# ConvFFN 0's shift and scale and the spectrum's cross products on VectorE, the sums in other steps

## The chip, the cores and the metric

The kernel runs on one core of a Trainium2 chip. The metric is the device time of one execution in microseconds; the figure for the kernel before is the median of three runs.

A core has TensorE (PE in the profile; its weight loads are PEld), VectorE (DVE), ScalarE (ACT), GpSimd (POOL) and SyncE (SP), which here only issues DMAs. Each engine works through its own queue in order.

## What is computed

The reference is two layers over 512 tokens of width 1024, in float32. Layer 0 mixes by a Hyena long convolution (512 channels) beside neighbourhood attention (8 heads of 64, with 256 context tokens); layer 1 by a Conformer convolution. Each is followed by a ConvFFN, and each sub-layer is wrapped in norms with shift, scale and gate computed from a conditioning vector:

```
def adaln_params(cond, w_mod, b_mod):
    m = jax.nn.silu(cond) @ w_mod + b_mod
    return jnp.split(m[:, None, :], 6, axis=-1)
...
    shift1, scale1, gate1, shift2, scale2, gate2 = adaln_params(c, w_mod[layer], b_mod[layer])
    ...
    h = h + gate1 * rms_norm(y, g_mix_post[layer])
    hn = rms_norm(h, g_ffn_pre[layer]) * (1 + scale2) + shift2
    y = conv_ffn(hn, ffn_w_up[layer], ffn_w_dw[layer], ffn_b_dw[layer], ffn_w_down[layer])
...
def bidirectional_fft_conv(v, h_fwd, h_bwd, bias):
    ...
    v_f = jnp.fft.rfft(v.astype(jnp.float32), n=n, axis=1)
    k_f = jnp.fft.rfft(k_full, n=n, axis=0)
    y = jnp.fft.irfft(v_f * k_f[None], n=n, axis=1)[:, :length]
```

The change concerns `shift2` and `scale2` of layer 0 and the complex product `v_f * k_f`.

## The kernel before

**Numbers.** Every float32 product of weight and activation is made of three matmuls (`mm3`, lines 296 to 299) from a high and a low part of each operand. `split` (lines 311 to 316) makes the two parts of a loaded weight: ScalarE copies the high part (L314), VectorE subtracts it (L315).

**Loads.** Weights are read 512 KB at a time by `load` (line 306, DMA issued by SP at L308) into a pool `raw` of three buffers, and split into a pool `w` of eight; a `Stream` asks for the loads and splits some units ahead. The same three `raw` buffers take the loads of the background work.

**Stages around the change,** as the program is written: four key projections (`k_proj`, TensorE, keys evicted by L975 on ScalarE and L976 on VectorE) with two spectra between them (`fdft`); the value projection (four weights of 512 KB, two of them followed by the load and split of an inverse-transform table `ti`); the inverse transform (`py`, L1096 and L1098 on VectorE); two of the four query projections; then the attention, 16 units (`a_scores`, `a_exp`, `a_norm`, `a_T`, `a_split`, `a_pv`), with the other two query projections in it. GpSimd adds the bias tiles (L1135) and scales the softmax (L1180) there. The output projection and the second stage's transposes (L537), which use the ConvFFN's shift and scale (L548), follow.

**The spectrum's product** (`prod` in `fdft`, lines 992 to 1020): ScalarE copies the odd half from PSUM (L994, L995), VectorE forms sums and differences `v` (L998 to L1001), and for each of two halves the product with the filter's spectrum is two instructions of 128x1024: the cross product `tm` (L1007) on GpSimd, the direct one `yy` (L1008) on VectorE. VectorE combines them (L1011, L1012, L1017) and ScalarE and VectorE split the result (L1018, L1019).

**The shift and scale** (`mod_cols`, lines 455 to 473, which runs `gemv_acc`, lines 431 to 453) is a generator that advances only when `bg_step` is called. For layer 0 it has 27 steps: one load; 16 steps which each issue the next load and add one loaded block, times a column of SiLU(c), to `acc`; eight empty steps; one with 16 small matmuls `pm` (L465); one for the columns (L469 to L471). With `side=True` the block is scaled by ScalarE into a tile `gt` (L446) and added by GpSimd (L448); otherwise VectorE does both in one instruction (L452), as for the other layer and the gates. The steps are called three at a time: twice before and once after the second key projection, after each later key projection, after the second spectrum, and after each of the four weights of the value projection, so that all 27 are called before the inverse transform.

**What sets the order.** The program is handed to a scheduler that gives each engine's queue its order by a simulated timeline, with the written order as priority; a buffer is granted when the last reader of the tile in it is done. Only TensorE's order in the prologue is written out by hand.

Of the kernel before, what the change touches and what calls it, by code (L numbers as in the profile page):

```python
# [10 lines left out]
F32 = mybir.dt.float32  # L11
F32R = mybir.dt.float32r
AF = mybir.ActivationFunctionType
ALU = mybir.AluOpType
AX = mybir.AxisListType

P = 128
# [235 lines left out]
def backbone_kernel(ctx: ExitStack, tc: tile.TileContext, a, cols, out, dump=None, stop=None, mark=lambda s: None):  # L253
# [18 lines left out]
    def s4(dt=F32, shape=(P, 2, 512), n="s"):  # L272
        return spool.tile(list(shape), dt, name=nm(n), tag="s")
# [154 lines left out]

    MOD = {}

    def gemv_acc(src, n, cs, init=None, side=False):
        rs = []

        def ld(k):
            rs.append(load(src[k]))

        acc = s4(F32, (P, 1024), "acc")
        ld(0)
        yield None
        for k in range(n):  # L440
            if k < n - 1:
                ld(k + 1)
            ck_ = cs[:, k:k + 1]
            if side:
                t_ = acc if k == 0 else s4(F32, (P, 1024), "gt")
                A.activation(t_, rs[k], AF.Copy, bias=0.0, scale=ck_)  # L446
                if k:
                    G.tensor_tensor(acc, acc, t_, op=ALU.add)  # L448
            elif k == 0 and init is None:
                V.tensor_scalar(acc, rs[k], ck_, None, op0=ALU.mult)  # L450
            else:
                V.scalar_tensor_tensor(acc, rs[k], ck_, init if k == 0 else acc, op0=ALU.mult, op1=ALU.add)  # L452
            yield acc

    def mod_cols(l, whichs, side=False):

        n = 2 * len(whichs)
        acc = None
        for acc in gemv_acc(a[f"wcol{l}"], 8 * n, scn[n], side=side):
            yield  # L460
        for _ in range(8):
            yield
        pm = ps("pm")
        for m in range(8):
            PE.matmul(pm[:, n * m:n * m + n], acc[:, m * P:(m + 1) * P], sel[n], start=True, stop=True)  # L465
        yield
        for i, which in enumerate(whichs):
            B_, s_, A_ = col8(), col8(), col8()
            V.tensor_tensor(B_, pm[:, 2 * i:8 * n:n], pc(f"bsh{which}{l}"), op=ALU.add)  # L469
            V.tensor_tensor(s_, pm[:, 2 * i + 1:8 * n:n], pc(f"bsc{which}{l}"), op=ALU.add)  # L470
            V.scalar_tensor_tensor(A_, s_, 1.0, pc(f"gmp{l}" if which == 1 else f"gfp{l}"), op0=ALU.add, op1=ALU.mult)  # L471
            MOD[(l, which)] = (A_, B_)
        yield
# [27 lines left out]
    def bg_step(n=1):  # L501
        for _ in range(n):
            while bg:
                try:
                    next(bg[0])
                    break
                except StopIteration:
                    bg.pop(0)
# [442 lines left out]
                ctx_T()  # L951
        V.tensor_tensor(pp[i // 2][:, i % 2], got[0], got[1], op=ALU.mult)
    bg_drain()
    bg += [mod_cols(0, (2,), True)]


    mark("kproj")
# [24 lines left out]
    def fdft(fc):  # L982
        q4 = {}
        for par in (1, 0):
            for cs in range(2):
                pm = ps("pv")
                for hf in range(2):
                    ch = par * 2 + hf
                    mm3(pm, tfs(0, ch, cs, fc), tfs(1, ch, cs, fc), pT[0][:, ch], pT[1][:, ch], hf == 0, hf == 1)
                q4[(cs, par)] = pm  # L990

        def prod():
            od = s4(n="od")
            A.copy(od[:, 0], q4[(0, 1)])  # L994
            A.copy(od[:, 1], q4[(1, 1)])  # L995
            v0 = s4(n="v0")
            v1 = s4(n="v1")
            V.tensor_tensor(v0[:, 0], q4[(0, 0)], od[:, 0], op=ALU.add)  # L998
            V.tensor_tensor(v0[:, 1], q4[(1, 0)], od[:, 1], op=ALU.add)
            V.tensor_tensor(v1[:, 1], q4[(0, 0)], od[:, 0], op=ALU.subtract)  # L1000
            V.tensor_tensor(v1[:, 0], q4[(1, 0)], od[:, 1], op=ALU.subtract)  # L1001
            y = []
            for pr, v in ((0, v0), (1, v1)):
                kt = K[(fc, pr)]
                yy = s4(n="yy")
                tm = od if pr else s4(n="ytm")
                G.tensor_tensor(tm, v, kt[:, 1:2].broadcast_to([P, 2, 512]), op=ALU.mult)  # L1007
                V.tensor_tensor(yy, v, kt[:, 0:1].broadcast_to([P, 2, 512]), op=ALU.mult)  # L1008
                y.append((yy, tm))
            for yy, tm in y:  # L1010
                V.tensor_tensor(yy[:, 0], yy[:, 0], tm[:, 1], op=ALU.add)  # L1011
                V.tensor_tensor(yy[:, 1], yy[:, 1], tm[:, 0], op=ALU.subtract)  # L1012
            eh, el = p8(n="Eh"), p8(n="El")
            (y0, _), (y1, _) = y
            for j, (op, s) in enumerate(((ALU.add, 0), (ALU.add, 1), (ALU.subtract, 0), (ALU.subtract, 1))):
                X = (v0 if j < 2 else v1)[:, j % 2]
                V.tensor_tensor(X, y0[:, s], y1[:, 1 - s], op=op)  # L1017
                A.copy(eh[:, j], X)  # L1018
                V.tensor_tensor(el[:, j], X, f(eh[:, j]), op=ALU.subtract)  # L1019
            E[fc] = (eh, el)  # L1020
        return prod

    bg_step(3)
    ev0 = k_proj(0)
    p_T(3)
    bg_step(3)
    ev0()
    ev1 = k_proj(1)
    ev1()
    bg_step(3)  # L1030
    pr0 = fdft(0)
    pr0()
    mark("fdft")
    ev2 = k_proj(2)
    ev2()
    bg_step(3)
    ev3 = k_proj(3)
    ev3()
    bg_step(3)
    pr1 = fdft(1)  # L1040
    pr1()
    bg_step(3)


    mark("vproj")
# [2 lines left out]
    for kp in range(4):  # L1048
        wh, wl = ws.get(2, 2)
        for q in range(2):  # L1050
            kc = 2 * kp + q
            ns = slice(q * 512, (q + 1) * 512)
            for c in range(6):
                if c < 4:
                    sl = slice(c * P, (c + 1) * P)
                    ah, al = hk(hT, kc, 0, sl), hk(hT, kc, 1, sl)
                else:
                    sl = slice((c - 4) * P, (c - 3) * P)
                    ah, al = ck(kc, 0, sl), ck(kc, 1, sl)
                mm3(vacc[c], ah, al, wh[:, ns], wl[:, ns], kc == 0, kc == 7)  # L1060
        if kp in (1, 2):
            TI[kp - 1] = split(load(a["ti"][kp - 1]), None)
        bg_step(3)

    Vt = {}
    for c in range(6):
# [16 lines left out]
    for m in range(4):  # L1083
        py = ps("py")
        ms = slice(m * P, (m + 1) * P)
        for par in range(2):
            o = py[:, par * 256:(par + 1) * 256]
            for fc in range(2):
                for cs in range(2):
                    ns = slice(cs * 512 + par * 256, cs * 512 + par * 256 + 256)  # L1090
                    eh, el = E[fc]
                    j = par * 2 + cs
                    mm3(o, eh[:, j, ms], el[:, j, ms], TI[fc][0][:, ns], TI[fc][1][:, ns],
                        fc == 0 and cs == 0, fc == 1 and cs == 1)
        pi = pp[m // 2][:, m % 2]
        V.scalar_tensor_tensor(pi.rearrange("p (i e) -> p i e", e=2), pi.rearrange("p (i e) -> p i e", e=2),  # L1096
                               pc("hyb", m), py.rearrange("p (e i) -> p i e", e=2), op0=ALU.mult, op1=ALU.add)
        V.tensor_tensor(yh[m // 2][:, m % 2], pi, x0[m // 2][:, m % 2], op=ALU.mult)  # L1098

    mark("qproj")  # L1100

# [2 lines left out]
    def q_proj(pr):  # L1104
        u = ws.get(1, 2)
        pz = ps("pz")
        for kc in range(8):
            wh, wl = wst(u, kc)
            mm3(pz, wh, wl, hk(hT, kc, 0), hk(hT, kc, 1), kc == 0, kc == 7)
        t_, l_ = s4(F32R, n="qX"), s4(F32R, n="qL")  # L1110
        qX.append(t_)
        qL.append(l_)
        for e in range(2):
            G.memset(f(l_[HALF[1 - e], e]), 0.0)
        for e in range(2):
            src = pz[HALF[e]]
            for r in range(2):
                A.mul(t_[HALF[r], e], src, 0.125)
            V.scalar_tensor_tensor(l_[HALF[e], e], src, 0.125, f(t_[HALF[e], e]), op0=ALU.mult, op1=ALU.subtract)
# [104 lines left out]
    for u in range(16 + DV + 1):  # L1224
        if u < 16:
            a_scores(u)
            a_exp(u)
        if 2 <= u < 4:
            q_proj(u)
        if DN <= u < 16 + DN:  # L1230
            a_norm(u - DN)
        if DT <= u < 16 + DT:
            a_T(u - DT)
            a_split(u - DT)
        if DV <= u < 16 + DV:
            a_pv(u - DV)
        if u > DV and (u - DV) % 2 == 0:
            a_out((u - DV) // 2 - 1)
        if u == 2:
            v_shift()  # L1240
        if u % 4 < 2 and u < 12:
            bm_load(u // 4 * 2 + u % 4 + 2)
        if u % 4 in (1, 2) and u < 12:
            bm_make(u // 4 * 2 + u % 4 + 1)
# [305 lines left out]
```

## Time and profile before

| | before |
|---|---|
| median of 3 runs | 1291.08 us (1290.09 to 1294.53) |
| the profiled execution | 1290.61 us |
| its span, first to last instruction | 1288.8 us |
| busy: TensorE / VectorE / ScalarE / GpSimd | 1249.9 / 817.3 / 526.8 / 160.2 us |
| mean granted TensorE clock | 0.994 |
| chain that ended last | TensorE 76%, DMA 8%, VectorE 7%, ScalarE 4% |

The span is the part of an execution that the trace covers; the rest lies before the first and behind the last instruction. Times in the trace count from the span's start. A matmul's listed duration overlaps with the next one's, so TensorE's pace is read from the starts. Weight tiles are named `w`, the value projection's PSUM tiles `va`, the inverse transform's `py`, the key and query projections' `pz`.

### The profile page before, as it was taken

The numbers are of one execution on the slowest core, as the hardware profiler recorded it, in microseconds if no ns is written. First come the engines' busy times: TensorE is split into PE (matmuls) and PEld (weight loads), VectorE is DVE, ScalarE is ACT, GpSimd is POOL, SyncE is SP. The second block draws the span as 40 slices with busy tenths as digits, with TensorE's granted clock in tenths as the row PEclk, the third lists the DMA queues.
The fourth block names the chain that finished last, engine by engine and source line by source line (L and its number), as shares of the span: only waits on it lengthen the run. The fifth ranks groups of instructions, "written<-read, shape, count | busy, mean of one in ns | idle before, by whom it ended". The sixth has DMA issues, their size and how long they took to land.

```text
span 1288.8 us, 15592 instructions
## 1 busy us (share of the span) xinstructions
PE 1249.9 (97%) x6044; PEld 1027.3 (80%) x6044; DVE 817.3 (63%) x1068; ACT 526.8 (41%) x804; POOL 160.2 (12%) x198
## 2 busy tenths in 40 slices
PE   6999979999999999999999999999999999999997
PEld 3688867877898888878888887878888888888886
DVE  4577588476557888877825565686677555556233
ACT  5453543286435333243514433242544333345221
POOL 3210365283010000000000100101100000000001
PEclk9999998999999999999999999999999999999999
DMA  9536533342506477766336052040255333232321
GB/s 354 179 115 181 162 115 131 129 121 83 163 1 190 169 230 244 237 210 207 107 105 196 25 185 73 1 147 1 66 167 187 98 94 95 98 97 99 98 83 65
DMA packets 47818, 171.00 MB, mean 133 GB/s; under 512 B 5757, under 2 KB 5788, under 8 KB 47744
## 3 DMA queue, kind: packets, MB, share of 16 engines
q1 hardware_dynamic: 47092, 168.49, 39.9%
q0 software_dynamic: 464, 1.19, 0.4%
q8 instruction: 47, 0.77, 0.2%
q10 hardware_dynamic: 188, 0.33, 0.1%
q14 instruction: 27, 0.22, 0.1%
HBM read 167.10 MB, written 2.10 MB: 131 GB/s over the span
## 4 chain that ended last, share of the span: by engine, by line
PE 76%; DMA 8%; DVE 7%; ACT 4%; issue 3%; POOL 1%; SPq 0%; DVEq 0%; POOLq 0%; ACTq 0%
PE pz L297 12%; PE pz L298 12%; PE pz L299 12%; PE acc L297 8%; PE acc L298 8%; PE acc L299 8%; DMA raw<-in_wup 3%; DMA raw<-in_wcol 3%; DVE w L315 2%; PE pg L297 2%; PE pg L298 2%; PE pg L299 2%; ACT w L314 2%; PE po L1206 1%; PE pt L1186 1%
## 5 line engine op out<-in xcount | busy, mean ns | idle before, releaser
L299 PE MATMUL pz<-hTh,w 128*128 128x512 f32 (+1 forms) x920 | 345.2, 376 | 0.5 <-DVE w L315 0.5
L297 PE MATMUL pz<-hTh,w 128*128 128x512 f32 (+1 forms) x920 | 344.6, 377 | 0.9 <-DVE hTh L543 0.5
L298 PE MATMUL pz<-hTl,w 128*128 128x512 f32 (+1 forms) x920 | 345.4, 376 | 0.0
L315 DVE TENSOR_TENSOR w<-raw,w 128x1024 fp32r<-128x1024 f32 x159 | 201.1, 1268 | 211.1 <-ACT w L314 206.8
L314 ACT CAST w<-raw 128x1024 fp32r<-128x1024 f32 x159 | 166.3, 1051 | 345.5 <-PE pz L298 128.6
L299 PEld LDWEIGHTS pz<-hTh,w 128*128 128x128 f32 x920 | 173.8, 189 | 32.2 <-DVE w L315 1.0
L297 PEld LDWEIGHTS pz<-hTh,w 128*128 128x128 f32 x920 | 173.0, 189 | 31.5 <-DVE hTh L543 1.0
L298 PEld LDWEIGHTS pz<-hTl,w 128*128 128x128 f32 x920 | 173.9, 189 | 30.2 <-DVE hTl L544 0.4
L298 PE MATMUL acc<-w,gs 128*128 128x512 f32 x256 | 99.6, 389 | 0.0
L299 PE MATMUL acc<-w,gs 128*128 128x512 f32 x256 | 98.3, 389 | 0.0
L297 PE MATMUL acc<-w,gs 128*128 128x512 f32 x256 | 97.0, 389 | 0.0
L452 DVE SCALAR_TENSOR_TENSOR acc<-raw,sc,acc 128x1024 f32<-128x1024 f32 x59 | 75.6, 1281 | 28.6 <-DMA raw<-in_wgate 19.6
L416 POOL TENSOR_SCALAR t<-t,t 128x1 f32<-128x1 f32 x19 | 6.6, 348 | 636.6 <-ACT py L425 628.2
L901 ACT ACTIVATE cv<-pz,pk 128x512 f32<-128x512 f32 x88 | 67.6, 774 | 0.0
L903 DVE SCALAR_TENSOR_TENSOR cv<-pz,pk,cv 128x511 f32<-128x511 f32 x88 | 65.6, 747 | 1.8
L902 DVE SCALAR_TENSOR_TENSOR cv<-pz,pk,cv 128x511 f32<-128x511 f32 x88 | 65.2, 744 | 0.2 <-ACT cv L901 0.2
L1283 ACT ACTIVATE cv<-cv 128x512 f32<-128x512 f32 x44 | 27.7, 629 | 81.2 <-DVE cv L903 81.1
L297 PEld LDWEIGHTS acc<-w,gs 128*128 128x128 f32 x256 | 48.1, 188 | 10.1
L299 PEld LDWEIGHTS acc<-w,gs 128*128 128x128 f32 x256 | 48.1, 188 | 9.9
L298 PEld LDWEIGHTS acc<-w,gs 128*128 128x128 f32 x256 | 48.1, 188 | 9.9
L315 DVE TENSOR_TENSOR wk<-raw,wk 128x1024 fp32r<-128x1024 f32 x30 | 37.1, 1246 | 28.9 <-ACT wk L314 28.9
L558 DVE TENSOR_TENSOR py<-acc,gg 128x512 f32<-128x512 f32 x32 | 21.8, 688 | 48.4 <-ACT py L425 48.4
(334 smaller groups left out, 2050.2 us busy)
## 6 DMA issues: line engine op xcount, KB each, us to landing
raw<-in_wup SPq DMA_DIRECT2D x88, 512.0 KB, 3.6
raw<-in_wcol SPq DMA_DIRECT2D x48, 512.0 KB, 4.4
raw<-in_wdn SPq DMA_DIRECT2D x44, 512.0 KB, 3.6
raw<-in_wgate SPq DMA_DIRECT2D x32, 512.0 KB, 4.3
raw<-in_pw SPq DMA_DIRECT2D x24, 512.0 KB, 4.7
raw<-in_win SPq DMA_DIRECT2D x20, 512.0 KB, 3.6
land<-in_wmod SPq DMA_DIRECT2D x16, 512.0 KB, 10.2
raw<-in_wout SPq DMA_DIRECT2D x8, 512.0 KB, 3.6
```

Source lines behind the costliest of these rows:

```text
L297: PE.matmul(o, ah, bh, start=start, stop=False)
L298: PE.matmul(o, ah, bl, start=False, stop=False)
L299: PE.matmul(o, al, bh, start=False, stop=stop)
L314: A.copy(hi, r)
L315: V.tensor_tensor(lo, r, f(hi), op=ALU.subtract)
L452: V.scalar_tensor_tensor(acc, rs[k], ck_, init if k == 0 else acc, op0=ALU.mult, op1=ALU.add)
L558: V.tensor_tensor(p_[:, sl], y2[i], gg[:, sl], op=ALU.mult)
L901: A.activation(dst, pz, AF.Identity, bias=pc(bk, i), scale=pc(wk + "1", i))
L902: V.scalar_tensor_tensor(dst[:, 1:w], pz[:, 0:w - 1], pc(wk + "0", i), dst[:, 1:w], op0=ALU.mult, op1=ALU.add)
L903: V.scalar_tensor_tensor(dst[:, 0:w - 1], pz[:, 1:w], pc(wk + "2", i), dst[:, 0:w - 1], op0=ALU.mult, op1=ALU.add)
L1186: PE.transpose(b["pt"][:, c * P:(c + 1) * P], b["P"][:, c * P:(c + 1) * P], ident)
L1283: A.activation(cv[:, 0], cv[:, 0], AF.Silu, bias=0.0, scale=1.0)
```

## The change

ScalarE's and GpSimd's way of summing the shift and scale (`side`) is taken out, so that VectorE does each of the 16 sums in one instruction. The background steps are called at other places: two before the first key projection, one after it, one after each of the third and fourth, one after each weight of the value projection, two after each of the four parts of the inverse transform, one after each of the first two query projections as before, and one in each unit of the attention. The cross product of the spectrum goes from GpSimd to VectorE.

```
--- before.py
+++ after.py
@@ -428,7 +428,7 @@
 
     MOD = {}
 
-    def gemv_acc(src, n, cs, init=None, side=False):
+    def gemv_acc(src, n, cs, init=None):
         rs = []
 
         def ld(k):
@@ -441,22 +441,17 @@
             if k < n - 1:
                 ld(k + 1)
             ck_ = cs[:, k:k + 1]
-            if side:
-                t_ = acc if k == 0 else s4(F32, (P, 1024), "gt")
-                A.activation(t_, rs[k], AF.Copy, bias=0.0, scale=ck_)
-                if k:
-                    G.tensor_tensor(acc, acc, t_, op=ALU.add)
-            elif k == 0 and init is None:
+            if k == 0 and init is None:
                 V.tensor_scalar(acc, rs[k], ck_, None, op0=ALU.mult)
             else:
                 V.scalar_tensor_tensor(acc, rs[k], ck_, init if k == 0 else acc, op0=ALU.mult, op1=ALU.add)
             yield acc
 
-    def mod_cols(l, whichs, side=False):
+    def mod_cols(l, whichs):
 
         n = 2 * len(whichs)
         acc = None
-        for acc in gemv_acc(a[f"wcol{l}"], 8 * n, scn[n], side=side):
+        for acc in gemv_acc(a[f"wcol{l}"], 8 * n, scn[n]):
             yield
         for _ in range(8):
             yield
@@ -951,7 +946,7 @@
                 ctx_T()
         V.tensor_tensor(pp[i // 2][:, i % 2], got[0], got[1], op=ALU.mult)
     bg_drain()
-    bg += [mod_cols(0, (2,), True)]
+    bg += [mod_cols(0, (2,))]
 
 
     mark("kproj")
@@ -1004,7 +999,7 @@
                 kt = K[(fc, pr)]
                 yy = s4(n="yy")
                 tm = od if pr else s4(n="ytm")
-                G.tensor_tensor(tm, v, kt[:, 1:2].broadcast_to([P, 2, 512]), op=ALU.mult)
+                V.tensor_tensor(tm, v, kt[:, 1:2].broadcast_to([P, 2, 512]), op=ALU.mult)
                 V.tensor_tensor(yy, v, kt[:, 0:1].broadcast_to([P, 2, 512]), op=ALU.mult)
                 y.append((yy, tm))
             for yy, tm in y:
@@ -1020,26 +1015,24 @@
             E[fc] = (eh, el)
         return prod
 
-    bg_step(3)
+    bg_step(2)
     ev0 = k_proj(0)
     p_T(3)
-    bg_step(3)
+    bg_step(1)
     ev0()
     ev1 = k_proj(1)
     ev1()
-    bg_step(3)
     pr0 = fdft(0)
     pr0()
     mark("fdft")
     ev2 = k_proj(2)
     ev2()
-    bg_step(3)
+    bg_step(1)
     ev3 = k_proj(3)
     ev3()
-    bg_step(3)
+    bg_step(1)
     pr1 = fdft(1)
     pr1()
-    bg_step(3)
 
 
     mark("vproj")
@@ -1060,7 +1053,7 @@
                 mm3(vacc[c], ah, al, wh[:, ns], wl[:, ns], kc == 0, kc == 7)
         if kp in (1, 2):
             TI[kp - 1] = split(load(a["ti"][kp - 1]), None)
-        bg_step(3)
+        bg_step(1)
 
     Vt = {}
     for c in range(6):
@@ -1096,6 +1089,7 @@
         V.scalar_tensor_tensor(pi.rearrange("p (i e) -> p i e", e=2), pi.rearrange("p (i e) -> p i e", e=2),
                                pc("hyb", m), py.rearrange("p (e i) -> p i e", e=2), op0=ALU.mult, op1=ALU.add)
         V.tensor_tensor(yh[m // 2][:, m % 2], pi, x0[m // 2][:, m % 2], op=ALU.mult)
+        bg_step(2)
 
     mark("qproj")
 
@@ -1227,6 +1221,7 @@
             a_exp(u)
         if 2 <= u < 4:
             q_proj(u)
+        bg_step(1)
         if DN <= u < 16 + DN:
             a_norm(u - DN)
         if DT <= u < 16 + DT:
```

## Rows read from the trace of the kernel before

**Rows 1.** Stretches: length; PE, PEld, DVE, ACT, POOL busy (instructions); clock, DMA share, GB/s.

```profile
131.00:181.20 50.20, 50.09 (x266) 42.83 (x265) 31.78 (x34) 22.60 (x31) 26.21 (x10) 1.00 0.45 142
181.20:230.20 49.00, 38.38 (x160) 30.64 (x161) 41.48 (x41) 20.38 (x26) 24.80 (x11) 0.90 0.40 130
230.20:246.70 16.50, 13.54 (x98) 13.10 (x97) 6.77 (x8) 4.92 (x8) 0.32 (x1) 0.90 0.22 77
...
257.60:325.00 67.40, 65.66 (x509) 52.03 (x509) 47.94 (x135) 51.07 (x111) 38.38 (x52) 1.00 0.30 99
```

**Rows 2.** TensorE's waits from 131 to 232 and 232 to 327 us: total, times, longest.

```profile
PE va L297 <- ACT w L314: 5.1, 1, 5.1
PE va L298 <- DVE w L315: 3.8, 1, 3.8
PE va L297 <- DVE kX L976: 1.4, 1, 1.4
...
PE py L297 <- ACT w L314: 2.1, 1, 2.1
...
PE py L298 <- DVE w L315: 0.9, 1, 0.9
```

**Rows 3.** Timeline of TensorE: start us, us, line, operation; idle before in brackets.

```profile
158.69 0.39 PE L297 MATMUL pz<-hTh,w 128*128 128x512 f32 x1
...
180.71 0.39 PE L299 MATMUL pv<-pTh,TFl 128*128 128x512 f32 x1
...
220.18 1.95 PE L465 MATMUL pm<-sel,acc 128*128 128x2 f32 x16 [0.49 <-POOL acc L448]
...
246.75 0.40 PE L297 MATMUL pz<-hTh,w 128*128 128x512 f32 x1
```

**Rows 4.** Chain that ended last, from 150 to 262 us: start us, us, what.

```profile
236.04 0.21 PE py L297
...
239.71 0.12 PE py L297
...
246.91 0.23 PE pz L297
```

**Rows 5.** Timeline of VectorE, 168 to 225 us (columns as in rows 3).

```profile
168.16 6.39 DVE L1008 TENSOR_TENSOR yy<-v,K 128x1024 f32<-128x1024 f32 x2
...
212.05 1.21 DVE L1008 TENSOR_TENSOR yy<-v,K 128x1024 f32<-128x1024 f32 x1
...
217.80 4.67 DVE L1017 TENSOR_TENSOR v<-yy,yy 128x512 f32<-128x512 f32 x4
222.40 2.49 DVE L1019 TENSOR_TENSOR El<-v,Eh 128x512 fp32r<-128x512 f32 x4
```

**Rows 6.** Timeline of GpSimd, around 168 us.

```profile
167.72 2.40 POOL L1007 TENSOR_TENSOR ytm<-v,K 128x1024 f32<-128x1024 f32 x1
```

**Rows 7.** ScalarE's waits from 131 to 232 us: total, times, longest.

```profile
ACT gt L446 <- DMA raw<-in_wcol: 13.5, 5, 4.7
```

**Rows 8.** Timeline of ScalarE, around 190 us.

```profile
189.54 1.04 ACT L314 CAST w<-raw 128x1024 fp32r<-128x1024 f32 x1
```

**Rows 9.** Costliest groups: line, engine, operation, count; busy us, mean ns; idle before.

```profile
L452 DVE SCALAR_TENSOR_TENSOR acc<-raw,sc,acc 128x1024 f32<-128x1024 f32 x59 | 75.6, 1281 | 28.6 <-DMA raw<-in_wgate 19.6
```

**Rows 10.** Line 452 by itself: what its engine waited for (us, times).

```profile
  DMA raw<-in_wcol: 8.3, 6
```

**Rows 11.** Groups by line of VectorE, 158.7 to 213.8 us (columns as in rows 9).

```profile
L976 DVE TENSOR_TENSOR kX<-pz,kX 64x512 fp32r<-64x512 f32 x5 | 3.4, 690 | 0.2
...
L976 DVE TENSOR_TENSOR kcX<-px,kcX 64x256 fp32r<-64x256 f32 x6 | 2.5, 421 | 0.1
```

**Rows 12.** DMA issues: count, KB each, median us to landing.

```profile
raw<-in_wcol SPq DMA_DIRECT2D x48, 512.0 KB, 4.4
```

**Rows 13.** Chain that ended last, whole span: start us, us, what.

```profile
359.43 1.31 PE pt L537 x12
```

**Rows 14.** Line 1180 by itself: duration ns least/median/most, first and last start.

```profile
L1180 POOL TENSOR_SCALAR P<-P,t x32: 685/695/1732, 264.6 to 315.2; 128x512 f32<-128x512 f32 x32
```

More of the change, by code (lines that the diff above doesn't have):

```diff
@@ L429, in backbone_kernel, with gemv_acc @@
     MOD = {}
-    def gemv_acc(src, n, cs, init=None, side=False):
+    def gemv_acc(src, n, cs, init=None):
         rs = []
@@ L443, in gemv_acc @@
             ck_ = cs[:, k:k + 1]
[L444 to L449, printed above, removed]
+            if k == 0 and init is None:
                 V.tensor_scalar(acc, rs[k], ck_, None, op0=ALU.mult)
@@ L453, in gemv_acc, with mod_cols @@
             yield acc
-    def mod_cols(l, whichs, side=False):
+    def mod_cols(l, whichs):
         n = 2 * len(whichs)
         acc = None
-        for acc in gemv_acc(a[f"wcol{l}"], 8 * n, scn[n], side=side):
+        for acc in gemv_acc(a[f"wcol{l}"], 8 * n, scn[n]):
             yield
@@ L953, in backbone_kernel @@
     bg_drain()
-    bg += [mod_cols(0, (2,), True)]
+    bg += [mod_cols(0, (2,))]
     mark("kproj")
@@ L1006, in prod @@
                 tm = od if pr else s4(n="ytm")
-                G.tensor_tensor(tm, v, kt[:, 1:2].broadcast_to([P, 2, 512]), op=ALU.mult)
+                V.tensor_tensor(tm, v, kt[:, 1:2].broadcast_to([P, 2, 512]), op=ALU.mult)
                 V.tensor_tensor(yy, v, kt[:, 0:1].broadcast_to([P, 2, 512]), op=ALU.mult)
@@ L1021, in fdft @@
         return prod
-    bg_step(3)
+    bg_step(2)
     ev0 = k_proj(0)
     p_T(3)
-    bg_step(3)
+    bg_step(1)
     ev0()
@@ L1029, in backbone_kernel @@
     ev1()
-    bg_step(3)
     pr0 = fdft(0)
@@ L1035, in backbone_kernel @@
     ev2()
-    bg_step(3)
+    bg_step(1)
     ev3 = k_proj(3)
     ev3()
-    bg_step(3)
+    bg_step(1)
     pr1 = fdft(1)
     pr1()
-    bg_step(3)
     mark("vproj")
@@ L1062, in backbone_kernel @@
             TI[kp - 1] = split(load(a["ti"][kp - 1]), None)
-        bg_step(3)
+        bg_step(1)
     Vt = {}
@@ L1098, in backbone_kernel @@
         V.tensor_tensor(yh[m // 2][:, m % 2], pi, x0[m // 2][:, m % 2], op=ALU.mult)
+        bg_step(2)
     mark("qproj")
@@ L1229, in backbone_kernel @@
             q_proj(u)
+        bg_step(1)
         if DN <= u < 16 + DN:
```

## The prediction

> **What bounds the kernel now.** I read the table of stretches first. From 131 to 181.2 us and again in the attention TensorE is busy nearly all the time at full clock; in the second stretch, the value projection, it is busy 38.4 of 49.0 us at a mean clock of 0.90, and in the third, the inverse transform, 13.5 of 16.5 us at 0.90 [rows 1]. So the two stretches from 181 to 247 us are where time can be had, and both lie in the steps that the change touches. The next view, TensorE's waits there, names the cause: five waits of 5.1, 3.8, 1.4, 2.1 and 0.9 us, 13.3 us together, all for ScalarE's or VectorE's half of a weight split or for the eviction of keys [rows 2].
>
> The third view gives the whole loss, clock included. From the last transform matmul (start 180.71 us, so the next could start at 180.94) to the first query matmul at 246.75 us are 65.8 us [rows 3]. In it TensorE has 144 matmuls of 512 columns, each 0.23 us of the chain at full clock, 96 of 256 columns at 0.12 [rows 4], and the 16 small `pm` matmuls, under 2 us: 144 x 0.2275 + 96 x 0.12 + 1.8 = 46.1 us. **Lost: 19.7 us.** The waits named, with 0.5 before `pm`, are 13.8 of them; most of the rest is clock: after a wait the inverse transform's matmuls count 0.21 instead of 0.12 [rows 4], which is the lower of the clock's two levels (1.2 instead of 2.4 GHz).
>
> Why are the splits late? Fourth view, VectorE's own instructions. A product `yy` of 128x1024 takes 1.21 us alone, and two of them 6.39 while GpSimd works; four `v` of 128x512 take 4.67 where four instructions of their size take 2.49 alone [rows 5]. The pair of `yy` began at 168.16, when GpSimd's `ytm` product (167.72, 2.40 us) was under way [rows 6]. I count nine such lengthenings, from this one to that at 217.80 us (a merged group of four counts once): 4.0 + 2.2 + 2.2 + 2.1 + 1.4 + 2.2 + 2.2 + 2.2 + 2.2, about 21 us of VectorE time. ScalarE adds its part: it stood 13.5 us in five waits for the modulation's loads [rows 7], with copies of the spectrum and splits behind them in its queue; the second value weight was copied only at 189.54 us [rows 8], and TensorE's longest wait ends there.
>
> **The change part by part.** (1) ScalarE loses 16 scalings and its waits for those loads; GpSimd loses 15 additions, which reach TensorE only through the lengthenings and the 0.5 us before `pm`.
>
> (2) VectorE gains 16 sums of 1.28 us [rows 9], 20.5 us; the first is a plain multiplication, which I price no lower. Some of them wait for their load: six such waits elsewhere took 8.3 us, 1.4 each [rows 10].
>
> (3) VectorE gains the four cross products, 4 x 1.21 = 4.8 us, GpSimd loses them. Parts 2 and 3 add 25.3 us, and the lengthenings give some 21 back: VectorE's total hardly moves. What moves is when: the old steps put all 16 sums ahead of the inverse transform, the new ones sums 0 to 3 in the key projections, 4 to 7 in the value projection, 8 to 15 in the inverse transform.
>
> (4) VectorE's budget up to the inverse transform. With TensorE unbroken the transform starts at 180.9 + 32.8 = 213.7 us. From 158.7, when the first spectrum is in PSUM and the third key projection starts [rows 3], VectorE then has 55.0 us for: two spectrum products of 14.8 us (sixteen at 2.49 / 4, four at 1.21 [rows 5]), 29.6; two key evictions of two 0.69 and two 0.42 [rows 11], 4.4; six splits, 128x1024 like a product, 7.3; sums 1 to 7, 9.0, and 1.4 of waiting before each, 9.8. That is 60.1, **5.1 us too much**. I take 3.6 as the residue of lost TensorE time, because the last sum and its wait (2.7) can partly come after the splits; the bounds are 0 (the waits hide) and the 13.8 us of today's waits.
>
> (5) Loads. Every step issues one 512 KB load on SP's queue through the three `raw` buffers. At the end of the value projection two of the three hold query weights 2 and 3, which are split only late, so loads 9 to 15 go through one buffer: 4.4 us to landing [rows 12], 1.3 for the sum, 0.3 to issue, 6.0 us each. Seven take 42 us. Nobody needs the result until the second stage's transposes, at 359 us in the old chain [rows 13], so I cost the lateness itself at nothing; if that cover went it would be paid once. Query weight 3 and the output weights queue behind them on SP, as do the bias tiles; the price of that is between 0 and one load, 4.4 us, and I take 0, as for the other lateness.
>
> (6) The attention. Up to five sums fall behind its start. VectorE is busy 47.9 of 67.4 us there [rows 1], so there is room, but each sum also meets GpSimd. Here the row shows only that GpSimd's softmax scaling takes 0.69 us and at most 1.73 [rows 14]: a meeting costs about 1.0. Five sums cost between 0 and 5 x (1.28 + 1.73) = 15.0 us, as if each stood alone and met a scaling of the longest kind; I take 1.5, one or two meetings. The Trainium skill, "SBUF — State Buffer", section "Who interferes with whom", says that a VectorE instruction with two SBUF inputs and a GpSimd instruction that reads SBUF lock each other out for the whole instruction, and the sum is of that kind. By that rule alone every meeting costs the rest of the other's instruction, and the term would be nearer the upper end; the trace agrees with it in the product at 168.16, but has no such sum beside GpSimd.
>
> (7) `pm` costs the same 1.8 us in the attention as before; its result is not waited for. The 15 `gt` buffers go and `acc` is held until attention unit 6: nothing, between one buffer less for attention and 15 more before it.
>
> Sum: -19.7 + 3.6 + 1.5 = **-14.6 us**. The profiled execution's own time is 1290.61 us (1288.8 span and 1.8 around it), 0.5 below the median shown. 1290.6 - 14.6 = 1276.0.
>
> **The rivals.** A, the forecast: the waits from 181 to 247 us mostly go and little comes back, -10 to -20 us, 1270 to 1281. For it: every TensorE wait there ends in a VectorE or ScalarE instruction that sits behind what is removed. Chance 0.62.
>
> B: VectorE becomes the bound of the value projection. Its queue is over-full by part 4, and one late load holds up splits behind a waiting sum, as ScalarE's waits do today. Half or more of the 13.8 us of waits stays, and the lower clock behind them: -4 to -9 us, 1282 to 1287. Against it: only seven sums, not fifteen, lie there. Chance 0.18.
>
> C: the gain is given back in the attention, each sum locking out GpSimd's scaling or bias addition, by the upper bound of part 6: -19.7 + 3.6 + 15.0, about -1 us, 1290. By the Trainium skill's rule in part 6 it would come so if the meetings are many. The same end would come if the change did not do what it says, and the splits waited for weight buffers rather than for their engines; against that, by its place in ScalarE's queue the second value weight's copy came right behind the keys' eviction, which came behind the spectrum product. Chance 0.09.
>
> D, slower: VectorE's queue is in order, and the sums 9 to 15 stand in it ahead of the attention's first maxima. By part 5 the last one ends at 213.7 + 42 + 1.3 = 257 us, while the attention could start at 213.7 + 96 x 0.12 + 48 x 0.23 = 236: 21 us that TensorE cannot fill. -14.6 + 21 = +6 us, 1297. It decides from the third such sum on (2.5 x 6.0 us eat the gain). For it: the sums are written ahead of the attention, with one free buffer. Against it: each engine's order comes from a simulated timeline, which can put a maximum before a sum whose load is late. Chance 0.11.
>
> **How the numbers follow.** A measurement of this kernel can tell about 0.3%, 3.9 us, from no change. Faster by more: A and B, 0.80. Within: C, 0.09. Slower: D, 0.11. The range reaches from A's lower end, 1270, to 1289, past B into the edge of C; it leaves out D, most of C and A's extreme, about 0.2.
>
> **What the new profile would show.** Right: the `yy` and `v` instructions of the spectrum product all near their minimum; no TensorE wait over 2 us from 181 to 247; clock 1.00 in the value projection; the first query matmul at 228 to 236 us; VectorE sums at 1.28 us into the early attention with 1 to 3 us of waiting each. Wrong: waits for a split of value weights as long as before (B); GpSimd's scaling often above 1.2 us and `pt` waiting for it (C); maxima that start late, right behind sums waiting for their load (D).

## The result and the profile after

The changed kernel takes 1275.18 us (median of 4 runs, 1273.64 to 1275.87) against 1290.59 for the kernel before on the same chip (4 runs): ratio 0.9875, 95% interval 0.9850 to 0.9899, or 15.4 us by the medians. The profiled execution took 1275.04 us, 1273.2 of it span, 15.6 less than the span before.

The table of stretches of the changed kernel (columns as in [rows 1]; the stretches are cut where its stages now begin):

```profile
131.00:181.20 50.20, 50.20 (x268) 43.23 (x268) 40.96 (x53) 20.36 (x34) 0.00 (x0) 1.00 0.34 101
181.20:213.70 32.50, 32.50 (x145) 26.93 (x144) 24.47 (x32) 9.02 (x13) 1.04 (x2) 1.00 0.47 142
213.70:230.20 16.50, 16.50 (x120) 15.62 (x119) 10.40 (x12) 3.09 (x5) 1.57 (x3) 1.00 0.55 172
...
246.70:257.60 10.90, 7.60 (x32) 6.39 (x33) 10.46 (x20) 7.17 (x14) 7.84 (x12) 0.84 0.85 248
```

The value projection fills 32.5 of 32.5 us on TensorE at full clock, where it filled 38.4 of 49.0 at 0.90 [rows 1]. GpSimd does nothing from 131 to 181 us. A new gap stands in the attention's front: TensorE is busy 7.6 of 10.9 us from 246.7 at a mean clock of 0.84; the two waits for `pt` below, 3.4 us, make up that gap.

TensorE's waits from 131 to 320 us, all of them, against the five of [rows 2] (and 1.7 us for `pt` in the kernel before):

```profile
PE pt L1180 <- POOL P L1174: 3.4, 2, 2.4
PE sc L1153 <- ACT PT L1188: 0.5, 1, 0.5
```

Where the time came from is read off three starts in TensorE's timeline: the first value, query and output projection matmul. Changed kernel:

```profile
181.64 0.39 PE L297 MATMUL va<-w,hTh 128*128 128x512 f32 x1
...
225.79 0.40 PE L297 MATMUL pz<-hTh,w 128*128 128x512 f32 x1
...
306.01 0.50 PE L297 MATMUL acc<-w,yH 128*128 128x512 f32 x1
```

In the kernel before, the first of the output projection:

```profile
322.17 0.50 PE L297 MATMUL acc<-w,yH 128*128 128x512 f32 x1
```

From the end of the spectrum to the query projection were 65.8 us [rows 3]; they are 225.79 - 181.64 = 44.2, with the 1.8 us of `pm` gone elsewhere: 65.8 - 1.8 - 44.2 = **19.8 us gained**, all that was lost there. From the query to the output projection were 322.17 - 246.75 = 75.4 us; they are 80.2, of which 1.8 is `pm`: **3.0 us given back**. The stretch starts 0.7 us later and the rest of the kernel takes 0.6 longer: -19.8 + 3.0 + 1.3 = -15.5, the span's 15.6.

VectorE's timeline in the changed kernel:

```profile
162.53 1.22 DVE L1002 TENSOR_TENSOR ytm<-v,K 128x1024 f32<-128x1024 f32 x1
163.66 1.22 DVE L1003 TENSOR_TENSOR yy<-v,K 128x1024 f32<-128x1024 f32 x1
...
178.02 1.28 DVE L447 SCALAR_TENSOR_TENSOR acc<-raw,sc,acc 128x1024 f32<-128x1024 f32 x1
...
213.53 1.29 DVE L447 SCALAR_TENSOR_TENSOR acc<-raw,sc,acc 128x1024 f32<-128x1024 f32 x1 [3.85 <-DMA raw<-in_wcol]
...
237.34 4.20 DVE L447 SCALAR_TENSOR_TENSOR acc<-raw,sc,acc 128x1024 f32<-128x1024 f32 x2 [0.56 <-DMA raw<-in_wcol]
...
241.58 0.69 DVE L1166 CUSTOM_DVE_ANT_1 P<-sc,BM 128x512 f32<-128x512 f32 x1
```

Every product is at its 1.22 us (against [rows 5]). From 213.5 us on the sums stand waiting for their loads, and two of them, 4.20 us together instead of 2.6, stand right ahead of the attention's first maximum. The chain that ended last shows the cause there: load and sum in turn, as part 5 had it.

```profile
226.95 4.83 DMA raw<-in_wcol
231.78 0.02 issue
231.81 1.29 DVE acc L447
233.10 0.02 issue
233.12 4.12 DMA raw<-in_wcol
...
237.34 2.89 DVE acc L447
```

The sum at 237.34 took 2.89 us because GpSimd had begun a bias addition 0.04 us earlier (its timeline):

```profile
237.30 1.84 POOL L1129 TENSOR_TENSOR BM<-BM,mask 128x768 f32<-128x768 f32 x1
```

### The profile page after: what moved, and what is told of

Its sections match the earlier page's. It is cut to its first block, busy times and chain, and to the rows that moved or that the text cites. A ratio compares the mean times of both kernels' runs of the same rounds, so it can differ in the third digit from the quotient of the medians.

```text
span 1273.2 us, 15549 instructions
## 1 busy us (share of the span) xinstructions
PE 1245.8 (98%) x6044; PEld 1025.6 (81%) x6044; DVE 821.2 (64%) x1088; ACT 509.9 (40%) x788; POOL 112.2 (9%) x179
## 4 chain that ended last, share of the span: by engine, by line
PE 83%; DMA 7%; DVE 5%; ACT 2%; issue 2%; POOL 1%; DVEq 0%; POOLq 0%; ACTq 0%
PE pz L297 12%; PE pz L299 12%; PE pz L298 12%; PE acc L297 8%; PE acc L299 8%; PE acc L298 8%; DMA raw<-in_wcol 3%; DMA raw<-in_wup 3%; PE pg L297 2%; PE pg L298 2%; PE pg L299 2%; DVE acc L447 1%; DVE w L315 1%; PE po L1200 1%; ACT w L314 1%
## 5 line engine op out<-in xcount | busy, mean ns | idle before, releaser
L315 DVE TENSOR_TENSOR w<-raw,w 128x1024 fp32r<-128x1024 f32 x159 | 195.4, 1232 | 195.5 <-ACT w L314 192.7
L447 DVE SCALAR_TENSOR_TENSOR acc<-raw,sc,acc 128x1024 f32<-128x1024 f32 x74 | 96.9, 1309 | 44.0 <-DMA raw<-in_wcol 25.2
```

The lines of the kernel that those rows point to most:

```text
L315: V.tensor_tensor(lo, r, f(hi), op=ALU.subtract)
```

## The experiments

All twelve runs, as ratio to the kernel before, measured beside them on the same chip:

| run | ratio (95% interval) | median us |
|---|---|---|
| e1_cross | 0.9971 (0.9954 to 0.9988) | 1288.00 |
| e2_sums_oldsteps | 0.9908 (0.9879 to 0.9936) | 1279.88 |
| e3_side_newsteps | 1.0006 (0.9989 to 1.0023) | 1291.28 |
| e4_cross_back | 0.9907 (0.9879 to 0.9935) | 1279.43 |
| e5_no_gpsimd | 0.9865 (0.9840 to 0.9889) | 1274.41 |
| e6_last_sums_out | 0.9844 (0.9822 to 0.9866) | 1271.08 |
| e7_own_buffers | 0.9880 (0.9858 to 0.9903) | 1276.30 |
| e8_old_steps_both | 0.9858 (0.9836 to 0.9880) | 1273.18 |
| after_again | 0.9873 (0.9852 to 0.9894) | 1273.75 |
| e9_spread_short | 0.9873 (0.9851 to 0.9895) | 1274.06 |
| e10_ti_earlier | 0.9901 (0.9884 to 0.9919) | 1277.62 |
| e11_idle_gpsimd | 1.0040 (1.0026 to 1.0055) | 1296.72 |

The medians before were 1290.26 (e1 to e4), 1291.11 (e5 to e8), 1290.41 (the next three) and 1291.89 us (e11). "The lock" stands below for what the prediction read from [rows 5]: VectorE's instructions become longer beside GpSimd's.

**The parts, one at a time.** First the cross products alone, on the kernel before.

```
-                G.tensor_tensor(tm, v, kt[:, 1:2].broadcast_to([P, 2, 512]), op=ALU.mult)
+                V.tensor_tensor(tm, v, kt[:, 1:2].broadcast_to([P, 2, 512]), op=ALU.mult)
```

> The kernel before with the four cross products on VectorE and nothing else. Theory (waits come from GpSimd's lock and from ScalarE's queue standing for the modulation's loads): the four yy fall from 11.0 to 4.9 us in all, but the sums keep both causes, so only part of the 19.7 us comes back: -2 to -7 us, and the waits of TensorE for the value weights' splits stay at 5 us or more. Rival (the lock on the cross products alone makes the splits late): those waits go and -12 us or more. Rival (VectorE's time decides): 4.8 us added to VectorE, no gain or slower.

Measured -2.3 us. TensorE's waits from 131 to 330 us fell only from 15.5 to 11.4 us in all, and two of them are new:

```profile
PE va L297 <- DVE kcX L976: 4.8, 2, 3.7
PE pm L465 <- POOL acc L448: 4.7, 1, 4.7
```

The two long waits for the second value weight are gone, so that part of the theory's expectation missed, but a wait for a key eviction on VectorE and one for GpSimd's own additions take their place.

The sums alone, on the kernel before:

```
-    bg += [mod_cols(0, (2,), True)]
+    bg += [mod_cols(0, (2,))]
```

> The kernel before with the 16 sums done by VectorE alone, the steps where they were and the cross products on GpSimd. Theory: ScalarE stands for no load any more and 15 of 19 GpSimd instructions go, so most waits go: -8 to -14 us; what stays is VectorE standing for loads ahead of the spectrum's instructions. If the spread of the steps is what matters (16 sums and their loads ahead of the inverse transform are too many for VectorE and the raw buffers): -5 us or less, with VectorE's waits for the modulation's loads of 10 us or more before 230 us. No sum falls into the attention, so its start is as in the kernel before: 65 to 68 us from the first query matmul of the attention's front to the output projection.

Measured -10.4 us, within the theory's range; this part is the larger. VectorE stood 5.9 us for these loads from 131 to 230 us, under the 10 of the rival. From the first query matmul to the output projection it takes 76.2 us, near the 75.4 of the kernel before and not the 65 to 68 put down.

The changed kernel with the old way of summing, at the new steps:

```
+            if side:
+                t_ = acc if k == 0 else s4(F32, (P, 1024), "gt")
+                A.activation(t_, rs[k], AF.Copy, bias=0.0, scale=ck_)
+                if k:
+                    G.tensor_tensor(acc, acc, t_, op=ALU.add)
...
-    bg += [mod_cols(0, (2,))]
+    bg += [mod_cols(0, (2,), True)]
```

> The changed kernel with the sums again scaled by ScalarE and added by GpSimd, at the new step positions; the cross products on VectorE. Theory: fewer loads stand before the inverse transform, so ScalarE's standing falls, but each GpSimd addition (2.4 us) still locks VectorE out; and eight additions now fall beside the bias additions and the softmax: 3 to 8 us slower than the changed kernel, 1278 to 1283, part of it in the attention. If the step positions were all, it equals the changed kernel within 2 us.

It missed by 8 us: the whole gain is gone, by another way than the one foreseen. TensorE's waits from 131 to 330 us:

```profile
PE sc L1158 <- ACT qX L1117: 16.8, 1, 16.8
```

and ScalarE's from 225 to 260 us:

```profile
ACT gt L446 <- DMA raw<-in_wcol: 18.2, 8, 4.3
```

The value projection had no wait at all here, though GpSimd's additions still met VectorE there: a split took 3.43 us instead of 1.22, and a pair of additions 11.50 instead of 4.8 (timelines of VectorE and of GpSimd):

```profile
171.07 3.43 DVE L315 TENSOR_TENSOR w<-raw,w 128x1024 fp32r<-128x1024 f32 x1
```

```profile
194.06 11.50 POOL L448 TENSOR_TENSOR acc<-acc,gt 128x1024 f32<-128x1024 f32 x2 [13.48 <-ACT gt L446]
```

Spread out as they are here, the additions cost TensorE nothing there. But eight scalings, each waiting for its load, stood in ScalarE's queue ahead of the queries' copies, and the attention could not begin: 16.8 us in one piece. That is rival D's mechanism at full size, on ScalarE instead of VectorE.

The changed kernel with the cross products back on GpSimd:

```
-                V.tensor_tensor(tm, v, kt[:, 1:2].broadcast_to([P, 2, 512]), op=ALU.mult)
+                G.tensor_tensor(tm, v, kt[:, 1:2].broadcast_to([P, 2, 512]), op=ALU.mult)
```

> The changed kernel with the cross products back on GpSimd. Theory: yy rises from 1.2 to about 3.2 us three times of four, cross product and yy in turn, each spectrum product some 5 us longer; VectorE has 8.8 us free before the inverse transform, so TensorE loses 0 to 4 us: 1275 to 1279. If the lock of the cross products was the main cause: 1285 or more.

1279.43, just over the expected end: 4.3 us for four GpSimd instructions. TensorE's longest wait is now at the attention, for a query on VectorE:

```profile
PE sc L1154 <- DVE qL L1113: 4.0, 1, 4.0
```

**Is the spread of the steps worth anything?** Sums and cross products on VectorE, steps left as they were:

```
-    bg += [mod_cols(0, (2,), True)]
+    bg += [mod_cols(0, (2,))]
...
-                G.tensor_tensor(tm, v, kt[:, 1:2].broadcast_to([P, 2, 512]), op=ALU.mult)
+                V.tensor_tensor(tm, v, kt[:, 1:2].broadcast_to([P, 2, 512]), op=ALU.mult)
```

> The kernel before with the sums and the cross products on VectorE and the steps where they were, that is the changed kernel without the spread. Sums on VectorE alone gave -10.4, and the cross products gave 4.3 us in the changed kernel. If the parts add: 1275 to 1277, equal to the changed kernel, and the spread is worth nothing. If the spread is needed once VectorE carries both (45 us of sums and products ahead of the inverse transform): 1279 to 1283, with TensorE waiting for splits or evictions before 225 us. No sum falls into the attention.

1273.18 us, ratio 0.9858: even with the changed kernel, and somewhat under the 1275 to 1277 expected. Alone the two parts gave 2.3 and 10.4, together 17.9: they help each other. The likely reason is that either of them, left on GpSimd, still lengthens VectorE's instructions (in e2 the four `yy` take 2.3 us on average). The spread is worth nothing that these runs can tell, and in two more pairs that differ in the steps alone it gains nothing either: e2 and e4 (1279.88 and 1279.43), e1 and e3 (1288.00 and 1291.28). In the last pair the spread does move the time. From the first value to the first query matmul are 62.3 us in e1 (8.1 of them `pm` and the wait before it) and 46.1 in e3 (TensorE's timelines, e1 first), but what was won there is lost in e3's wait of 16.8 us.

```profile
182.64 0.39 PE L297 MATMUL va<-w,hTh 128*128 128x512 f32 x1
...
244.94 0.40 PE L297 MATMUL pz<-hTh,w 128*128 128x512 f32 x1
```

```profile
181.72 0.39 PE L297 MATMUL va<-w,hTh 128*128 128x512 f32 x1
...
227.85 0.40 PE L297 MATMUL pz<-hTh,w 128*128 128x512 f32 x1
```

In e8 VectorE does all 16 sums before the inverse transform (the last one in its timeline):

```profile
202.37 1.28 DVE L452 SCALAR_TENSOR_TENSOR acc<-raw,sc,acc 128x1024 f32<-128x1024 f32 x1
```

and what remains is the late second table, TensorE's wait in the inverse transform:

```profile
PE py L297 <- ACT w L314: 1.7, 1, 1.7
```

**Lock or ScalarE's queue?** The kernel before with cross products and additions on VectorE, the scaling left on ScalarE with its waits, the steps where they were:

```
-                    G.tensor_tensor(acc, acc, t_, op=ALU.add)
+                    V.tensor_tensor(acc, acc, t_, op=ALU.add)
...
-                G.tensor_tensor(tm, v, kt[:, 1:2].broadcast_to([P, 2, 512]), op=ALU.mult)
+                V.tensor_tensor(tm, v, kt[:, 1:2].broadcast_to([P, 2, 512]), op=ALU.mult)
```

> The kernel before with GpSimd out of the stretch: cross products and the 15 additions on VectorE, but the scaling still on ScalarE and the steps where they were. It keeps ScalarE's standing for the loads (13.5 us before) and takes the lock away; VectorE gets 15 additions of 1.2 us and four products. If the lock is the larger cause: -8 us or more. If ScalarE's place in the queue is (as the run with sums on VectorE and the cross products left suggests, -10.4): 0 to -5 us, with ScalarE still idle 10 us or more for the loads and TensorE waiting 5 us or more for weights or evictions that ScalarE makes.

1274.41 us: the whole gain, with ScalarE standing for the loads as long as before ([rows 7] had 13.5). Its waits from 131 to 232 us:

```profile
ACT gt L446 <- DMA raw<-in_wcol: 13.1, 8, 5.0
```

Yet it copied the second value weight 10.9 us earlier than in the kernel before ([rows 8]; its timeline):

```profile
178.63 1.03 ACT L314 CAST w<-raw 128x1024 fp32r<-128x1024 f32 x1
```

VectorE's groups from 131 to 240 us, now 1.2 us each (the columns of [rows 9]):

```profile
L448 DVE TENSOR_TENSOR acc<-acc,gt 128x1024 f32<-128x1024 f32 x15 | 18.3, 1222 | 9.7 <-ACT gt L446 9.5
...
L1008 DVE TENSOR_TENSOR yy<-v,K 128x1024 f32<-128x1024 f32 x4 | 4.8, 1216 | 0.0
```

The lock decides: with it gone, ScalarE's waits cost nothing. What they cost beside the lock was not run by itself. The reverse: GpSimd put back into e8 with additions that nobody waits for.

```
+            if idle:
+                if k == 0:
+                    dm = s4(F32, (P, 1024), "dm")
+                    G.memset(dm, 0.0)
+                G.tensor_tensor(dm, dm, rs[k], op=ALU.add)
```

> Sums and cross products on VectorE, old steps (1273.2), plus a GpSimd addition of 128x1024 for each of the 16 loaded blocks, into a tile that nobody reads; it only occupies GpSimd and its SBUF reads at the places of the old additions. If VectorE's being locked out by GpSimd is what the gain came from: VectorE's 128x1024 subtractions and products go to 2.2 us and more again, and the time rises by 5 to 14 us, 1278 to 1287, though no instruction waits for GpSimd's result. If it was the chain of dependences (sum after scaling, spectrum behind both) or ScalarE's queue: 1272 to 1275. The loaded buffers are held 1 to 2 us longer, which alone should cost under 2 us.

1296.72 us, 23.5 more than e8 by the medians and well past the 1287 expected, slower than the kernel before. VectorE's groups from 131 to 240 us:

```profile
L452 DVE SCALAR_TENSOR_TENSOR acc<-raw,sc,acc 128x1024 f32<-128x1024 f32 x15 | 33.8, 2253 | 1.4 <-DMA raw<-in_wcol 1.2
...
L1012 DVE TENSOR_TENSOR od<-v,K 128x1024 f32<-128x1024 f32 x2 | 6.8, 3419 | 0.0
```

and the stretch of the value projection in the table of stretches:

```profile
181.20:214.00 32.80, 17.82 (x68) 14.20 (x67) 32.42 (x33) 8.92 (x16) 10.08 (x4) 0.74 0.35 112
```

A sum takes 2.25 us on average instead of 1.28, VectorE is busy 32.4 of 32.8 us and TensorE 17.8. TensorE's longest wait ends at a key eviction in VectorE's queue:

```profile
PE va L297 <- DVE kX L981: 15.0, 1, 15.0
```

The run overstates the case, because each addition starts on the same landing as the sum of its block, so that the two often meet, and because it holds the loaded buffers longer. That share was not separated, but it is not what held VectorE: its sums stood 1.2 us for their loads. A second TensorE wait, 2.9 us for a value weight that landed late, may belong to it.

**What the attention's front lost.** The changed kernel without loads and sums 9 to 15, so that this part of the shift and scale is left out:

```
-        for acc in gemv_acc(a[f"wcol{l}"], 8 * n, scn[n]):
+        for acc in gemv_acc(a[f"wcol{l}"], 8 * n if l else 9, scn[n]):
             yield
+        if l == 0:
+            for _ in range(7):
+                yield
```

> The changed kernel without the last seven loads and sums (9 to 15) of the ConvFFN 0 shift and scale, steps kept empty; that part of the computation is left out. Theory: what the attention's start lost (query to output projection 3.5 us longer than before, without pm) is those sums in VectorE's queue ahead of the first maxima, and their loads: -3 to -5 us against the changed kernel, 1270 to 1272, first exponential 3.5 to 4.5 us after the last of the first queries' matmuls instead of 5.6. Rival (the attention lost because TensorE came earlier than its bias tiles and masks could): no difference beyond 1 us.

1271.08 us, 4.1 below the changed kernel. Its first output projection matmul and first exponential:

```profile
303.17 0.50 PE L297 MATMUL acc<-w,yH 128*128 128x512 f32 x1
```

```profile
241.04 0.72 ACT L1171 ACTIVATE P<-P,t 128x512 f32<-128x512 f32 x1
```

That exponential comes 3.8 us behind the end of the first queries' matmuls, against 5.6 in the changed kernel, as the theory had it. Its query projection begins at 226.35, so that query to output takes 76.8 us, 75.0 without `pm`: the 75.4 of the kernel before. The late sums, with their loads, are the 3.0 us given back.

Three attempts to keep them out. Buffers of their own for the loads:

```
+            if own:
+                r = s4(F32, (P, 1024), "own")
+                SP.dma_start(r, src[k])
+                rs.append(r)
+            else:
+                rs.append(load(src[k]))
```

> The changed kernel with the loads of ConvFFN 0's shift and scale in buffers of the large pool s instead of the three raw ones. Theory (sums fall into the attention because load and sum go in turn through one free raw buffer): sums 9 to 15 end before the attention's first maximum and VectorE waits less for these loads than the 25.2 us of the changed kernel; -2 to -4 us, 1271 to 1273. Rival (the pool s is full in the attention's front, so extra buffers push its tiles back): same or slower by up to 3 us.

1276.30, no gain. The sums do come earlier, all before the first maximum, and VectorE's waits for loads of this kind (layer 1's included) fall from 25.2 to 12.7 us, but the last of them fares badly (timeline of VectorE, and of GpSimd at that place):

```profile
232.70 6.73 DVE L452 SCALAR_TENSOR_TENSOR acc<-own,sc,acc 128x1024 f32<-128x1024 f32 x1
```

```profile
232.95 5.39 POOL L1134 TENSOR_TENSOR BM<-BM,mask 128x768 f32<-128x768 f32 x3
```

Beside three bias additions in a row, 5.39 us, one sum took 6.73 us, and the queries behind it were late (TensorE waited 3.4 us for `qL`). So neither theory held as put: the waits went, and the lock took their place.

The spread ended with the value projection (three steps after each of its weights, none in the inverse transform):

```
-        bg_step(1)
+        bg_step(3)
...
-        bg_step(2)
```

> The changed kernel with three steps after each weight of the value projection and none in the inverse transform, so that 17 steps are written before the transform as it starts (the spread ends there). Theory (the spread past the transform costs, by sums in the attention's front): the attention starts as in the kernel without the last sums, and TensorE may wait 0 to 4 us for the second inverse-transform table: 1271 to 1275, 0 to 4 us faster than the changed kernel. Rival (sums now come between splits in the value projection): TensorE waits for a value weight, slower than the changed kernel.

1274.06 us beside 1273.75 of the changed kernel on the same chip (after_again): the same, where 0 to 4 us less was expected. The attention did not start as without the last sums; the loads were still late and TensorE waited for a query on VectorE:

```profile
PE sc L1153 <- DVE qL L1112: 3.1, 1, 3.1
```

> The changed kernel once more, beside the two that follow on the same chip: 1273.5 to 1276, ratio 0.987 to 0.989.

Measured 1273.75 us, ratio 0.9873.

And e8 with the two tables loaded one weight earlier:

```
-        if kp in (1, 2):
-            TI[kp - 1] = split(load(a["ti"][kp - 1]), None)
+        if kp in (0, 1):
+            TI[kp] = split(load(a["ti"][kp]), None)
```

> Sums and cross products on VectorE, old steps (1273.2 before), with the two inverse-transform tables loaded and split after the first and second value weights instead of the second and third. Theory (what is left there is the second table's load, 1.7 us of waiting and the lower clock behind it): the wait goes, -1.5 to -3.5 us, 1269.5 to 1272, a gain on the changed kernel of 3 to 6 us. Rival (the tables' place pushes the query weights back): no TensorE wait at the transform but one at the first query projection, and no gain.

1277.62 us, 3.9 us slower than the changed kernel on the same chip, where a gain of 3 to 6 was expected. The scheduler put inverse-transform matmuls among those of the value projection, and TensorE waited there (its timeline):

```profile
209.74 0.58 PE L297 MATMUL py<-w,Eh 128*128 128x256 f32 x1 [2.36 <-ACT w L314]
```

No version clearly beats the changed kernel; e8, the simplest, equals it. 1271.1, the time without the late sums, is the nearest to a floor that was seen.

## Why the prediction was right, point by point

The forecast of 1276.0 and the measured 1275.18 lie 0.8 us apart, and the case that came is A. Its terms, though, are right only in part.

- **The loss of 19.7 us, recovered:** right in place and size; 19.8 us came back, with the clock at 1.00.
- **The residue of 3.6 us (part 4):** mis-sized; it was 0. I charged VectorE with seven sums and 1.4 us of waiting before each between 158.7 and 213.7 us. Five ran there, the last from 213.5, with 0.5 and 3.9 us of waiting instead of 9.8; the first two had run at 143 and 148 us. It looks as if the scheduler set a sum where it expected its load and put other work before it. VectorE was busy 46.3 of 55.1 us, not over-full. Rival B fell with it.
- **The attention's 1.5 us (part 6):** too small; 3.0 us net of `pm`, by e6. Part 5's chain of load and sum ran as described, and part of it was paid: two sums, one of them lengthened to 2.89 us, stood ahead of the first maximum. Rivals C and D are both seen there, small: the lock at 237.3 us, the queue from 213 to 241. The sums being in VectorE's queue cost 3 us; in ScalarE's (e3) the same loads cost TensorE 16.8 us in one wait.
- The two errors, -3.6 and +1.5, and 1.3 us elsewhere that I had left out nearly cancel: -14.6 was said, -15.5 came. That the forecast came within 0.8 us is therefore partly luck.
- **Why the splits are late:** the lock was right, by e5 and e11. ScalarE's part was wrong: with its waits kept and the lock gone, all the gain came, and ScalarE copied the second value weight at 178.63 us (e5) instead of 189.54 [rows 8]. So that late copy came of VectorE's slow spectrum ahead of it.
- **"What moves is when" (part 3):** right as a description, but of no worth once VectorE does the sums: with the old steps the gain is the same (e8). What the spread saves at the inverse transform's table it pays in the attention.
- **The signs named beforehand** came, but for the sums' waits: products at their minimum, no TensorE wait over 2 us from 181 to 247, full clock, query projection at 225.8 (earlier than the 228 said). The sign of case C, `pt` waiting for GpSimd's scaling, came too, 2.4 us in one wait, but behind late maxima. The sums in the early attention were to wait 1 to 3 us each; the two at 237.34 waited 0.56 together, the three behind them not at all.

## What to carry to other kernels

Look at an instruction's spread of durations before its mean: the same VectorE shape at 1.2 and 3.2 us, with GpSimd busy beside the long ones, led to the cause here, while the longest wait that the trace listed named ScalarE, whose own waits cost nothing once the lock was gone (e5). Work given to GpSimd to relieve VectorE is not free when both read SBUF: taking back 25 us of it left VectorE's busy time nearly as it was (817.3 us before, 821.2 after). And background work that waits for loads is paid by what stands behind it in the same queue: ahead of the attention it cost 3.0 us on VectorE and a wait of 16.8 on ScalarE, ahead of the inverse transform, with the lock gone, nothing that shows on either (e8, e5).

## What the runs showed of the hardware

- A VectorE instruction can be kept waiting through more than one of GpSimd's: 6.73 us for a 1.28 us sum while GpSimd ran three additions back to back (e7). The reverse is seen too: two GpSimd additions of 2.4 us took 11.50 us from 194.06, while VectorE's instructions with two inputs in SBUF kept their shortest times up to 200 us: four `v` and four `El` in 2.49 us each (e3).
- VectorE instructions with one input in PSUM kept their 0.68 us beside GpSimd additions. In e11, VectorE's timeline, under two GpSimd additions that run from 168.31 to 174.07:

```profile
168.83 0.68 DVE L1004 TENSOR_TENSOR v<-pv,od 128x512 f32<-128x512 f32 x1
169.43 0.68 DVE L1006 TENSOR_TENSOR v<-pv,od 128x512 f32<-128x512 f32 x1
170.03 1.77 DVE L452 SCALAR_TENSOR_TENSOR acc<-raw,sc,acc 128x1024 f32<-128x1024 f32 x1
171.72 3.42 DVE L1012 TENSOR_TENSOR ytm<-v,K 128x1024 f32<-128x1024 f32 x1
```

The two with `pv` in PSUM are not lengthened, the two with both inputs in SBUF are. The Trainium skill, "SBUF — State Buffer", section "Who interferes with whom", names this difference: it counts VectorE's SBUF inputs, and an instruction with at most one of them, outside the two-port modes, does not contend. The trace agrees.
- The first step's multiplication, one input and a scalar, took 0.74 us where I had put 1.28.
